# Hybrid decoder block on one core: delta state in another pool, and activation rows padded by one element

## The chip, the cores and the metric

The kernel runs on one core of a Trainium2 chip. The metric is device time in microseconds of one execution. Before the change the median of three runs is 1653.5 us (1650.14 to 1654.55). Engines are named as in the profile: PE does matmuls, PEld its weight loads, DVE vector work, ACT activations and copies, POOL small work, SP issues the DMAs.

## The reference, cut to what matters

One layer on 256 tokens of width 2048, all in float32:

```
mod = silu(c) @ w_ada + b_ada                    # 2048 x 12288: sh1, sc1, gt1, sh2, sc2, gt2
hn  = rmsnorm(x) * (1 + sc1) + sh1
qkv, z, beta, a, glu, gate_a, gate_b = split(hn @ w_in)
A   = gated_delta_net(conv(qkv), beta, a) * silu(z) @ dn_w_o     # 8 heads of 128
B   = silu(layernorm(conv31(val * sigmoid(gl)))) @ cf_w_o        # conformer branch
x   = x + gt1 * ((sigmoid(gate_a) * A + sigmoid(gate_b) * B) @ w_out)
hn  = rmsnorm(x) * (1 + sc2) + sh2
x   = x + gt2 * ((silu(conv3(hn @ w_gate)) * (hn @ w_up)) @ w_down)
out = rmsnorm(x)
```

## The kernel before, in words

Every large product runs through `product` (L283). Its weights come in tiles `w` of 128 x 2 x 512 (512 KB, five buffers). ACT casts each to `wh` (L293), DVE makes the rest `wl` (L295), and PE runs three matmuls per weight slice and token half (L305 to L307): high by high, high by low, high by the weights' low part. The activations hn (later mg, the merged branches, and hn2) stay in one tile of 2 (high, low) x 16 x 256 per partition, and are the operand that PE loads as weights.

The order of the products is: p1 (a first part of all input projections), qkv, glu, gb, z, then **ga** (gate of branch A), **cfo** (`cf_w_o`), **dno** (`dn_w_o`), **out** (`w_out`), and the FFN products up1, gate, up, down. Between their matmuls lie smaller pieces that other bands of the program bring in: the delta rule for two halves of four heads (`delta`, L474), which has a chain of small matmuls and copies for each half, and the conformer's convolution (31 taps per channel on DVE and ACT, L417 to L428) with its layer norm (L758 to L781), which ends in the split `cfh`, `cfl` (L815, L816) that cfo reads.

The modulation `mod` is a side job: a load `ada_w` of one or two rows of `w_ada`, and a DVE sum `ada_acc += ada_w * c_act` (L166) for each. The blocks come in the order gt1 (two blocks of 16 loads of 512 KB), then sc2, sh2 in three parts each, then gt2. For gt1 and gt2 `ada_acc` starts as the bias row (a DMA, L149, after POOL's memset, L147), and PE turns the finished sum into a row with a matmul by ones (L174), which ACT copies to `gt` (L175). `ada_acc` has one buffer, so the next block begins when the last has been read. The side job advances by a credit per weight tile (`side_rate`), and each step is queued on SP behind the weight tile's load that gave it credit. `need` (L215) draws it to its end where a result is used: gt1 before out.

The tag `ada_w` in pool p0 has two buffers. In this order they hold the first q tile of the delta rule (`conv00`, L452), the delta state `St` of the first half (L636), `St` of the second half, and then all `ada_w` loads from gt1 on. The state is written once per half (L637) and read by L612 and L641. Pool pq holds the delta rule's own tiles, among them X0 and X1 (the solved values, L544), U0 and U1; after the delta rule these four tags hold the pieces of gt1 (L803).

A timeline simulation at build time, with bands of priority, sets the order of instructions on each engine; on the chip every engine runs its list in that order, and a buffer is given out in the program's order.

Of the kernel before, what the change touches and what calls it, by code (L numbers as in the profile page):

```python
# [8 lines left out]
F32 = mybir.dt.float32  # L9
F32R = mybir.dt.float32r  # L10
# [4 lines left out]
P = 128  # L15
D = 2048
S = 256
KD = D // P
# [37 lines left out]
def block_kernel(ctx: ExitStack, tc, x, vec, ab, rowv, w_ada, w_in, dn_w_o, cf_w_o, w_out, w_up, w_down, out):  # L56
# [6 lines left out]
    p0 = ctx.enter_context(tc.tile_pool(name="p0", bufs=1))  # L63
# [21 lines left out]
    def turn(out, in_, n=P):  # L85
        nc.tensor.transpose(out=out, in_=in_, identity=ident[0:n, 0:n])  # L86
# [138 lines left out]
    def rstd_col(ss):  # L225

        a = p0.tile([P, 2], F32, tag="nrm_a", name="nrm_a")
        nc.vector.tensor_reduce(out=a, in_=ss, axis=mybir.AxisListType.X, op=ALU.add)
        nc.gpsimd.tensor_scalar(out=a, in0=a, scalar1=1.0 / D, scalar2=EPS, op0=ALU.mult, op1=ALU.add)
        r = p0.tile([P, 2], F32, tag="nrm_c", bufs=3, name="nrm_c")  # L230
        nc.gpsimd.tensor_tensor(out=r, in0=a, in1=mhalf[:, 0:2], op=ALU.pow)
        return r
# [33 lines left out]
    def modulate(part):  # L266
        k0, k1 = R3[part]
        for k in range(k0, k1):
            i = slice(k - k0, k - k0 + 1)
            split(hn, k, x_sb[:, k, :], A1[part][:, i], mod[0][part][:, i])  # L270

    def turned(src, tiles, pool=ps, tag="tp"):

        bank = pool.tile([P, 2, S], F32, tag=tag, name="turned")
        for i, j in enumerate(tiles):
            for t in range(2):
                turn(bank[:, i, t * P:(t + 1) * P], src[:, t, j * P:(j + 1) * P])
        return bank
# [35 lines left out]
    def drain(it):  # L314
        for _ in it:
            pass
# [5 lines left out]
    with b_first():  # L322
        x_sb = p0.tile([P, KD, S], F32, tag="x", name="x_sb")
        xv = x.rearrange("(t p) n -> p t n", p=P)
        xt = p1.tile([P, 2, D], F32, tag="HS", name="xt")
        for q in range(2):
            for t in range(2):
                nc.sync.dma_start(out=xt[:, t, q * 1024:(q + 1) * 1024], in_=xv[:, t, q * 1024:(q + 1) * 1024])
        nc.sync.dma_start(out=vt, in_=vec)
        ss1 = p0.tile([P, 2, 2], F32, name="ss1")  # L330
        for q in range(2):
            for t in range(2):
                sq = p1.tile([P, 1024], F32, tag=("QA", "KA")[t], name="sq")
                nc.scalar.activation(out=sq, in_=xt[:, t, q * 1024:(q + 1) * 1024], func=AF.Square, accum_out=ss1[:, t, q:q + 1])
        r1 = rstd_col(ss1)
        for q in range(4):
            qs = slice(q * 512, (q + 1) * 512)
            for t in range(2):
                nc.vector.tensor_scalar(out=xt[:, t, qs], in0=xt[:, t, qs], scalar1=r1[:, t:t + 1], scalar2=None, op0=ALU.mult)
            for i in range(2):  # L340
                k = 4 * q + 2 * i
                nc.scalar.copy(out=x_sb[:, k:k + 2, :], in_=turned(xt, (k, k + 1), pd, f"dl{i}"))
        for j in (1, 0):
            drain(ada_block(j, 0, sup, 6, shared=True))
        hn = p0.tile([P, 2, KD, S], F32R, tag="hn", name="hn")
        modulate(0)
    hh, hl = (lambda k: hn[:, 0, k, :]), (lambda k: hn[:, 1, k, :])

# [44 lines left out]
    pq = mix.enter_context(tc.tile_pool(name="pq", bufs=1))  # L393
# [75 lines left out]
    def col(t, c, j, hb):  # L469

        i = c * H + hb * 4 + j
        return t[:, i:i + 1]

    def delta(hb, Q, K, Vt):  # L474
# [29 lines left out]
        def big(tag, c):  # L504
            return pq.tile([P, 4, P], F32, tag=f"{tag}{c}", name=f"{tag}{c}")

        def bank(c=""):
            if c == "":
                return ps.tile([P, 4, P], F32, tag="tp", name="bank")
            return pd.tile([P, 4, P], F32, tag=f"dl{c}", name="bank")  # L510

        def tok(c):
            return slice(c * P, (c + 1) * P)
# [93 lines left out]
        St = None  # L607
        for c in range(2):
            if c == 1:
                pt = bank(c)  # L610
                for j in range(4):
                    nc.tensor.matmul(pt[:, j, :], lhsT=K[:, j, tok(c)], rhs=St[:, j, :], start=True, stop=True, skip_group_check=True)  # L612
                for j in range(4):
                    nc.vector.scalar_tensor_tensor(out=X[c][:, j, :], in0=pt[:, j, :], scalar=col(eneg, c, j, hb), in1=X[c][:, j, :], op0=ALU.mult, op1=ALU.add)
            pt = bank(c)
            for j in range(4):
                nc.tensor.matmul(pt[:, j, :], lhsT=U[c][:, j, :], rhs=X[c][:, j, :], start=True, stop=True, skip_group_check=True)
            u = big("T", c)
            for j in range(4):
                nc.scalar.activation(out=u[:, j, :], in_=pt[:, j, :], func=AF.Copy, scale=br[:, c, j:j + 1])  # L620
            po = bank(c)
            for j in range(4):
                nc.tensor.matmul(po[:, j, :], lhsT=A[c][:, j, :], rhs=u[:, j, :], start=True, stop=True, skip_group_check=True)
            o = big("N", c)
            nc.scalar.copy(out=o, in_=po)
            if c == 0:
                pt = bank(c)
                for j in range(4):
                    turn(pt[:, j, :], K[:, j, tok(c)])
                kd = big("P", c)  # L630
                for j in range(4):
                    nc.scalar.activation(out=kd[:, j, :], in_=pt[:, j, :], func=AF.Copy, scale=kds[:, j:j + 1])
                pt = bank(c)
                for j in range(4):
                    nc.tensor.matmul(pt[:, j, :], lhsT=kd[:, j, :], rhs=u[:, j, :], start=True, stop=True, skip_group_check=True)
                St = p0.tile([P, 4, P], F32, tag="ada_w", bufs=2, name="St")  # L636
                nc.scalar.copy(out=St, in_=pt)  # L637
            else:
                pt = bank(c)
                for j in range(4):  # L640
                    nc.tensor.matmul(pt[:, j, :], lhsT=Q[:, j, tok(c)], rhs=St[:, j, :], start=True, stop=True, skip_group_check=True)  # L641
                for j in range(4):
                    nc.vector.scalar_tensor_tensor(out=o[:, j, :], in0=pt[:, j, :], scalar=col(eg, c, j, hb), in1=o[:, j, :], op0=ALU.mult, op1=ALU.add)

            sa = pq.tile([P, 4], F32, tag=f"sa{c}", name="sa")
            junk = big("P", c)
            for j in range(4):
                nc.scalar.activation(out=junk[:, j, :], in_=o[:, j, :], func=AF.Square, scale=so[:, c * 4 + j:c * 4 + j + 1], accum_out=sa[:, j:j + 1])
            nc.gpsimd.tensor_scalar(out=sa, in0=sa, scalar1=1.0 / P, scalar2=EPS, op0=ALU.mult, op1=ALU.add)
            sr = pq.tile([P, 4], F32, tag=f"sr{c}", name="sr")  # L650
            nc.gpsimd.tensor_tensor(out=sr, in0=sa, in1=mhalf[:, 0:4], op=ALU.pow)
            nc.gpsimd.tensor_tensor(out=sr, in0=sr, in1=so[:, c * 4:c * 4 + 4], op=ALU.mult)
            if c == 0:
                on = p1.tile([P, 2, 4, P], F32, tag=("KA", "KB")[hb], name="on")
            for j in range(4):
                nc.scalar.activation(out=on[:, c, j, :], in_=o[:, j, :], func=AF.Copy, scale=sr[:, j:j + 1])
# [92 lines left out]
    with b_delta():  # L749
        on0 = delta(0, *qa)  # L750
# [3 lines left out]
    with b_delta():  # L754
        on1 = delta(1, *qb)
# [67 lines left out]


    side_rate[0] = 0.7
    mg = p0.tile([P, 2, KD, S], F32R, tag="hn", name="mg")
    for g in range(4):
        def evac(pts, g=g):
            for pt, a, b in zip(pts, both(ga, g), both(gb, g)):
# [38 lines left out]
    gt_home[5] = lambda piece: p2.tile([P, 512], F32, tag=f"gt{piece}", name="gt2")  # L868
    with b_first():
        r2 = rstd_col(ss2)  # L870
    hn2 = p0.tile([P, 2, KD, S], F32R, tag="hn", name="hn2")

    def modulate2(part):
        k0, k1 = R3[part]
# [139 lines left out]
```

## Time and profile before

| | us |
|---|---|
| median of three runs | 1653.5 |
| profiled execution, own time | 1656.46 |
| its span, first to last instruction | 1654.8 |
| PE busy | 1530.3 (92%) |
| DVE busy | 1192.5 (72%) |
| ACT busy | 811.3 (49%) |
[...]

PE is busy 92% of the span. A matmul's end is modelled, and matmuls overlap, so a busy PE is not PE at its peak. Some records of matmuls are missing, so counts are a few per cent low in places. DVE and ACT make the split weights ahead of PE, with three buffers each for `wh` and `wl`.

### The profile page before, as it was taken

The numbers are of one execution on the slowest core, as the hardware profiler recorded it, in microseconds if no ns is written. First come the engines' busy times: TensorE is split into PE (matmuls) and PEld (weight loads), VectorE is DVE, ScalarE is ACT, GpSimd is POOL, SyncE is SP. The second block draws the span as 40 slices with busy tenths as digits, with TensorE's granted clock in tenths as the row PEclk, the third lists the DMA queues.
The fourth block names the chain that finished last, engine by engine and source line by source line (L and its number), as shares of the span: only waits on it lengthen the run. The fifth ranks groups of instructions, "written<-read, shape, count | busy, mean of one in ns | idle before, by whom it ended". The sixth has DMA issues, their size and how long they took to land. (4 is left out here: it accounts for less than half of the span.)

```text
span 1654.8 us, 20112 instructions
## 1 busy us (share of the span) xinstructions
PE 1530.3 (92%) x7198; PEld 1257.5 (76%) x7198; DVE 1192.5 (72%) x1556; ACT 811.3 (49%) x1223; POOL 56.4 (3%) x116
## 2 busy tenths in 40 slices
PE   5999999999999997906978999999999999999996
PEld 5887887888887876705867877888888887788885
DVE  5889868699998646846876889987544587755554
ACT  3553436777685644303435633455444444455443
POOL 2000001300021000000000000000000000000000
PEclk9999999999999999957999999999999999999998
DMA  9999765544544446876887988855556777665553
GB/s 341 384 360 356 234 198 145 153 127 138 164 144 132 136 149 208 276 257 220 276 294 264 308 294 291 291 178 175 181 190 196 255 233 246 226 188 183 185 184 101
DMA packets 182860, 366.59 MB, mean 222 GB/s; under 512 B 12516, under 2 KB 30948, under 8 KB 182632
## 3 DMA queue, kind: packets, MB, share of 16 engines
q1 hardware_dynamic: 182760, 365.31, 66.8%
q8 instruction: 56, 0.92, 0.2%
q14 instruction: 44, 0.36, 0.1%
HBM read 363.17 MB, written 2.10 MB: 221 GB/s over the span
## 5 line engine op out<-in xcount | busy, mean ns | idle before, releaser
L293 ACT CAST wh<-w 128x1024 fp32r<-128x1024 f32 x488 | 512.0, 1052 | 565.3 <-PE mm_up L306 133.1
L295 DVE TENSOR_TENSOR wl<-w,wh 128x1024 fp32r<-128x1024 f32 x488 | 593.7, 1222 | 269.3 <-ACT wh L293 267.6
L166 DVE SCALAR_TENSOR_TENSOR ada_acc<-ada_w,c_act,ada_acc 128x768 f32<-128x768 f32 (+2 forms) x236 | 242.9, 1030 | 119.6 <-DMA ada_w<-in_w_ada 113.6
L305 PE MATMUL mm_up<-wh,hn 128*128 128x512 f32 x472 | 185.7, 396 | 0.2 <-ACT hn L263 0.2
L306 PE MATMUL mm_up<-wh,hn 128*128 128x512 f32 x472 | 185.3, 393 | 0.0
L307 PE MATMUL mm_up<-wl,hn 128*128 128x512 f32 x472 | 172.9, 395 | 5.4 <-DVE wl L295 5.2
L305 PE MATMUL mm_down<-wh,h 128*128 128x512 f32 x352 | 139.9, 397 | 0.0
L306 PE MATMUL mm_down<-wh,h 128*128 128x512 f32 x352 | 139.7, 397 | 0.0
L307 PE MATMUL mm_down<-wl,h 128*128 128x512 f32 x352 | 126.4, 397 | 0.0
L305 PE MATMUL mm_p<-wh,hn 128*128 128x512 f32 x280 | 109.7, 395 | 2.1 <-ACT hn L263 2.0
L307 PEld LDWEIGHTS mm_up<-wl,hn 128*128 128x128 f32 x472 | 88.2, 188 | 27.4 <-DVE wl L295 9.4
L306 PE MATMUL mm_p<-wh,hn 128*128 128x512 f32 x280 | 109.0, 391 | 0.0
L305 PEld LDWEIGHTS mm_up<-wh,hn 128*128 128x128 f32 x472 | 89.1, 189 | 18.6 <-ACT hn L263 0.6
L306 PEld LDWEIGHTS mm_up<-wh,hn 128*128 128x128 f32 x472 | 88.7, 188 | 18.3 <-issue 0.5
L307 PE MATMUL mm_p<-wl,hn 128*128 128x512 f32 x280 | 98.7, 393 | 0.9 <-DVE wl L295 0.9
L305 PE MATMUL mm_gate<-wh,hn 128*128 128x512 f32 x232 | 91.3, 394 | 0.0
L306 PE MATMUL mm_gate<-wh,hn 128*128 128x512 f32 x232 | 90.6, 391 | 0.0
L307 PE MATMUL mm_gate<-wl,hn 128*128 128x512 f32 x232 | 85.1, 393 | 0.5 <-DVE wl L295 0.4
L307 PEld LDWEIGHTS mm_down<-wl,h 128*128 128x128 f32 x352 | 66.4, 189 | 16.1
L306 PEld LDWEIGHTS mm_down<-wh,h 128*128 128x128 f32 x352 | 66.4, 189 | 15.9
L305 PEld LDWEIGHTS mm_down<-wh,h 128*128 128x128 f32 x352 | 66.4, 189 | 15.8
L428 DVE SCALAR_TENSOR_TENSOR cfa<-u,vt,cfa 128x256 f32<-128x256 f32 x176 | 75.9, 481 | 0.3
(310 smaller groups left out, 2498.1 us busy)
## 6 DMA issues: line engine op xcount, KB each, us to landing
w<-in_w_up SPq DMA_DIRECT2D x176, 512.0 KB, 4.5
w<-in_w_in SPq DMA_DIRECT2D x130, 512.0 KB, 3.8
ada_w<-in_w_ada SPq DMA_DIRECT2D x96, 512.0 KB, 4.8
ada_w<-in_w_ada SPq DMA_DIRECT2D x128, 384.0 KB, 5.4
w<-in_w_down SPq DMA_DIRECT2D x88, 512.0 KB, 3.6
w<-in_w_in SPq DMA_DIRECT2D x64, 256.0 KB, 4.1
w<-in_w_out SPq DMA_DIRECT2D x32, 512.0 KB, 5.8
w<-in_cf_w_o SPq DMA_DIRECT2D x16, 512.0 KB, 3.5
```

The costliest lines, as they stand in the source:

```text
L166: nc.vector.scalar_tensor_tensor(out=acc[:, 0:n], in0=wt[:, i, :], scalar=c_act[:, k:k + 1], in1=acc[:, 0:n], op0=ALU.mult, op1=ALU.add)
L293: nc.scalar.copy(out=wh, in_=w)
L295: nc.vector.tensor_tensor(out=wl, in0=w, in1=wh.bitcast(F32), op=ALU.subtract)
L305: nc.tensor.matmul(pts[t], lhsT=xh(k)[:, ts], rhs=wh[:, kk, :], start=(k == k0), stop=False)
L306: nc.tensor.matmul(pts[t], lhsT=xl(k)[:, ts], rhs=wh[:, kk, :], start=False, stop=False)
L307: nc.tensor.matmul(pts[t], lhsT=xh(k)[:, ts], rhs=wl[:, kk, :], start=False, stop=(k == k1 - 1))
L428: nc.vector.scalar_tensor_tensor(out=acc[:, i, :], in0=us[g][:, i, k:k + S], scalar=V("cfconv", (2 * g + i) * CFK + k), in1=acc[:, i, :], ...
```

## The change

St is allocated from pool pq under the tag X0 and no longer from p0's `ada_w`. The tiles of hn, mg and hn2 get rows of 257 elements instead of 256, of which the first 256 are used.

```diff
-        hn = p0.tile([P, 2, KD, S], F32R, tag="hn", name="hn")
+        hn = p0.tile([P, 2, KD, S + 1], F32R, tag="hn", name="hn")[:, :, :, 0:S]
...
-                St = p0.tile([P, 4, P], F32, tag="ada_w", bufs=2, name="St")
+                St = pq.tile([P, 4, P], F32, tag="X0", name="St")
...
-    mg = p0.tile([P, 2, KD, S], F32R, tag="hn", name="mg")
+    mg = p0.tile([P, 2, KD, S + 1], F32R, tag="hn", name="mg")[:, :, :, 0:S]
...
-    hn2 = p0.tile([P, 2, KD, S], F32R, tag="hn", name="hn2")
+    hn2 = p0.tile([P, 2, KD, S + 1], F32R, tag="hn", name="hn2")[:, :, :, 0:S]
```

With it the order on the engines moves. SP's queue, at the bias row of gt1's first block (`ada_acc<-in_rowv`), before:

```order
L149 DMA ada_acc<-in_rowv 1x1024
L291 DMA w<-in_w_in 128x2x512 x30
L291 DMA w<-in_cf_w_o 128x2x512 x16
L291 DMA w<-in_dn_w_o 128x2x512 x3
L157 DMA ada_w<-in_w_ada 128x1024
L291 DMA w<-in_dn_w_o 128x2x512
```

And the same place now:

```order
L149 DMA ada_acc<-in_rowv 1x1024
L157 DMA ada_w<-in_w_ada 128x1024
L291 DMA w<-in_w_in 128x2x512 x2
L157 DMA ada_w<-in_w_ada 128x1024
L291 DMA w<-in_w_in 128x2x512 x2
L157 DMA ada_w<-in_w_ada 128x1024
```

The first `ada_w` stood behind 49 weight tiles, and now stands ahead of them; all 32 loads of gt1 lie between the weights of ga, cfo and the first of dno.

On PE, the step from dno to out before (`pt<-ada_acc` is the sum's matmul, `turned<-ident,gb` the transposes of the merged branches):

```order
L305 MATMUL mm_dno<-wh,oh_4863 128x512
L306 MATMUL mm_dno<-wh,ol_4864 128x512
L307 MATMUL mm_dno<-wl,oh_4863 128x512
L174 MATMUL pt<-ada_acc,ones 128x512 x2
L86 MATMUL turned<-ident,gb 128x128 x8
L305 MATMUL mm_out<-wh,mg 128x512 x2
```

The same matmul of that second block of gt1 now, at the step from cfo to dno:

```order
L307 MATMUL mm_cfo<-wl,cfh 128x512
L623 MATMUL bank<-T_4220,G_3878 128x128 x4
L174 MATMUL pt<-ada_acc,ones 128x512
L641 MATMUL bank<-St,conv_3569 128x128 x4
L174 MATMUL pt<-ada_acc,ones 128x512
L305 MATMUL mm_dno<-wh,oh_4845 128x512
```

The pair moved from the end of dno to its start, beside the last reads of St.

On PE, the first use of the layer norm's sum (`pt<-tot,ones_c`, L764) before, in the middle of ga:

```order
L307 MATMUL mm_ga<-wl,hn 128x512
L566 MATMUL bank<-T_3988,N_3842 128x64
L764 MATMUL pt<-tot,ones_c 128x256 x2
L566 MATMUL bank<-T_3988,N_3842 128x64 x3
L86 MATMUL bank<-ident,U_3914 128x128 x4
L305 MATMUL mm_ga<-wh,hn 128x512
```

And now the last rows between ga and cfo, which begin eight rows further up with that L764 (L776 and L251 are the norm's other matmuls, the rest are steps of the delta rule and the first block's L174):

```order
L584 MATMUL bank<-T_4064,N_3842 128x64 x4
L776 MATMUL pt_4277<-ones_c,sqs 128x1 x4
L584 MATMUL bank<-T_4083,N_3890 128x64 x4
L591 MATMUL bank<-U_3866,P_3871 64x64 x4
L251 MATMUL rb<-dg,ones 128x128 x2
L174 MATMUL pt<-ada_acc,ones 128x512
L591 MATMUL bank<-U_3914,P_3919 64x64 x4
L86 MATMUL bank<-ident,U_3866 64x64 x4
L174 MATMUL pt<-ada_acc,ones 128x512
L305 MATMUL mm_cfo<-wh,cfh 128x512 x2
```

The norm's matmuls stood among ga's, with nine more weight tiles of ga behind L764; now all of ga's matmuls stand ahead of them.

## Rows read from the trace of the kernel before

**Rows 1.** The page, busy tenths of the span in 40 equal slices:

```profile
PE   5999999999999997906978999999999999999996
```

**Rows 2.** Line L306: duration ns min/median/max, first and last start us, forms:

```profile
L306 PE MATMUL mm_ga<-wh,hn x128: 387/390/487, 458.4 to 581.1; 128*128 128x512 f32 x128
L306 PE MATMUL mm_out<-wh,mg x128: 388/390/775, 753.3 to 861.5; 128*128 128x512 f32 x128
...
L306 PE MATMUL mm_cfo<-wh,cfl x64: 390/397/484, 581.9 to 635.0; 128*128 128x512 f32 x64
...
L306 PE MATMUL mm_dno<-wh,ol x64: 391/398/775, 649.0 to 701.4; 128*128 128x512 f32 x64
```

**Rows 3.** Timeline of PE: start, us, line, out<-in, xcount [idle before <-releaser]:

```profile
647.37 1.97 PE L86 MATMUL bank<-ident,on 128*128 128x128 f32 x8 [5.58 <-DVE N L643]
...
746.34 3.78 PE L174 MATMUL pt<-ada_acc,ones 128*128 128x512 f32 x4 [44.29 <-DVE ada_acc L166]
...
773.67 1.09 PE L86 MATMUL pt<-ident,ada_acc 128*128 128x128 f32 x4 [9.22 <-DVE ada_acc L166]
...
873.22 1.97 PE L86 MATMUL turned<-ident,xn 128*128 128x128 f32 x8 [10.98 <-ACT xn L877]
```

**Rows 4.** Waits from 700 to 760: us in total, times, longest:

```profile
DVE ada_acc L166 <- DMA ada_w<-in_w_ada: 23.5, 13, 9.1
```

**Rows 5.** Timeline of SP's queue: start, us, what is issued, count:

```profile
481.93 70.25 SPq L291 DMA_DIRECT2D w<-in_w_in  x19
556.76 55.33 SPq L291 DMA_DIRECT2D w<-in_cf_w_o  x16
...
621.88 0.46 SPq L157 DMA_DIRECT2D ada_w<-in_w_ada  x1
...
712.83 44.70 SPq L157 DMA_DIRECT2D ada_w<-in_w_ada  x15
```

**Rows 6.** Busy us by stretch: PE, PEld, DVE, ACT, POOL, clock, DMA, GB/s:

```profile
512.00:572.00 60.00, 60.00 (x347) 52.08 (x346) 47.98 (x75) 36.18 (x60) 1.25 (x2) 1.00 0.43 132
...
641.00:702.00 61.00, 51.98 (x208) 40.72 (x208) 48.73 (x54) 22.25 (x34) 2.35 (x4) 0.92 0.77 253
...
752.00:863.00 111.00, 96.32 (x422) 77.67 (x420) 85.39 (x103) 43.42 (x67) 0.00 (x0) 0.94 0.81 266
...
1500.00:1600.00 100.00, 100.00 (x440) 81.26 (x440) 55.96 (x60) 45.45 (x55) 0.00 (x0) 1.00 0.57 186
```

**Rows 7.** Timeline of PE and DVE along the layer norm:

```profile
540.92 1.08 PE L764 MATMUL pt<-tot,ones_c 128*128 128x256 f32 x4
...
547.22 0.69 DVE L772 TENSOR_TENSOR sqs<-sqs 128x512 f32<-128x512 f32 x1
...
551.81 0.95 PE L776 MATMUL pt<-ones_c,sqs 128*128 128x1 f32 x8
...
553.79 0.29 DVE L250 TENSOR_SCALAR dg<-ident,nrm_r 128x128 f32<-128x128 f32 x1 [0.84 <-POOL nrm_r L243]
...
558.03 0.66 PE L251 MATMUL rb<-dg,ones 128*128 128x128 f32 x4
...
563.87 0.69 DVE L816 TENSOR_TENSOR cfl<-cfa,cfh 128x512 fp32r<-128x512 f32 x1 [1.99 <-ACT cfh L815]
```

**Rows 8.** The sum's group by form, and the landing time of `ada_w` loads:

```profile
L166 DVE SCALAR_TENSOR_TENSOR ada_acc<-ada_w,c_act,ada_acc 128x1024 f32<-128x1024 f32 x64 | 82.1, 1283 | 66.0 <-DMA ada_w<-in_w_ada 62.2 <-DMA ada_acc<-in_rowv 3.7
...
DMA to landing us min/median/max: 3.0/5.2/10.5
```

**Rows 9.** Operands off the raster, and hn's weight loads: ns min/median/max:

```profile
L428 DVE SCALAR_TENSOR_TENSOR cfa<-u,vt,cfa x176: 453/480/493, 333.2 to 536.7; 128x256 f32<-128x256 f32 x176
...
L409 ACT COPY u<-turned x4: 587/590/603, 329.2 to 336.1; 128x512 f32<-128x512 f32 x4
...
L570 PE MATMUL bank<-U,P x128: 217/275/276, 337.6 to 572.0; 128*128 128x64 f32 x128
...
L306 PEld LDWEIGHTS mm_up<-wh,hn x472: 187/188/193, 877.5 to 1526.6; 128*128 128x128 f32 x158
```

## The prediction

> **What bounds the kernel now.** I read the page first, then the table by stage, then the PE timeline where the page shows PE idle, then the waits and the DMA queue there. PE is the bound: it is busy nine tenths or more in nearly every slice, with one hole in slices 17 to 19 and a dent at 21 [rows 1]. In a full stretch 440 matmuls fill 100 us [rows 6], and nothing this change does makes PE's own work smaller, so the time can only come out of the hole.
>
> The stages around it are, by the first and last L306 matmul of each product: ga 458.4 to 581.1, cfo 581.9 to 635.0, dno 649.0 to 701.4, out 753.3 to 861.5 [rows 2]. Between dno and out PE stands still for 44.29 us until `ada_acc` is summed (L174 turns that sum into the row gt1), and in out again for 9.22 us for the next sum; before dno it waits 5.58 us for the delta rule, and before up1 10.98 us for the second norm [rows 3]. The 44 us are no lack of vector speed: inside them DVE itself waits 23.5 us, 13 times, for `ada_w` to land [rows 4]. It waits because all these loads come late. On the queue the weights of ga and cfo go out alone (19 and 16 loads in a row), the first `ada_w` only at 621.88, and then 15 `ada_w` stand ahead of the next `w_out` at 712.83 [rows 5]. Two buffers allow no more than two loads per landing (5.2 us median) plus the sum (1.28 us) [rows 8].
>
> The reason for 621.88: `St` of the second delta half is allocated from the same two-buffer tag ahead of these loads in program order, and it is written at the end of that half. The order of the changed program agrees: with St in another pool the first `ada_w` stands among the first ga weights.
>
> **The change part by part.** I call one weight tile with its 12 matmuls a chunk; ga has 32, cfo and dno 16 each, out 32. Own time of the profiled execution: 1656.5 us (span 1654.8 and 1.7 around it), 3 above the median 1653.5.
>
> A. *ga.* Sixteen `ada_acc` sums of the first gt1 block move into ga, sixteen of the second into cfo. DVE pays 16 x 1.2 = 19 us more in ga (1.28 each less the overlap with the next). By the new order four of them stand only one chunk behind the issue of their load, about 3 us against a landing of 5.2, so DVE also waits some 4 x 2.3 = 9 us with the next weights' split (L295) queued behind. DVE is 80% busy in 512 to 572 [rows 6], so ga's 124 us have 25 us free, and 9 us of layer norm leave ga: 28 against 34. That nearly fits, but the order is fixed and locally uneven: I take 5 us of PE waits, between 0 and 11.5. Against it PE work leaves ga: the norm's matmuls L764, L776, L251 (1.0 to 0.7 us each [rows 7]) and nine groups of four small delta matmuls at about 0.5 us (an estimate from those rows), 7.5 together. A = 5 - 7.5 = -2.5 (-7.5 to +4).
>
> B. *The wait that replaces the old one.* The sums are put among the conformer's taps, so the last tap and the layer norm's `tot` slip from ga's 23rd chunk behind its last. L764 now follows the last ga matmul, and cfo needs the norm's result: PE has little to run meanwhile. Before, the chain ran from 540.92 to the first `cfl` at 564.56 (563.87 + 0.69), hidden in ga. In it L776 stood 3.9 us behind its input (547.91 to 551.81) and L251 3.95 (554.08 to 558.03), behind ga matmuls that are gone now: 23.6 - 7.85 = 15.8 [rows 7]. Then one more thing: PE runs the two L174 of the first block just ahead of cfo, POOL clears `ada_acc` only after them, the bias row is loaded after that, and DVE's first sum of the second block waits for it with the second, third and fourth `cfl` queued behind. This delays cfo's second chunk by about 2 us. B = +17.8; at least 11 (without three splits of 1.2 to 1.5 that stood in the chain), at most 27 (chain not shortened, row later).
>
> C. *cfo.* PE comes out of B at the lower clock, as the 5.58 us gap brings the clock to 0.92 over 641 to 702 [rows 6]; the sums now pace DVE at (5.2 + 1.28)/2 = 3.2 us per load, and cfo's chunks take about 3.3 us on PE (53 us for 16 [rows 2]). +2.2 (0 to 6).
>
> D. *Tail of delta and dno.* The delta steps stand one to three chunks earlier relative to cfo, and six large sums no longer stand between the third and fourth split of dno. [...]
>
> E. *The 44.29 us.* Gone: the second block's last sum stands after cfo's 16th split, and its L174 before dno. With the L174 pair behind the wait (3.78 us, at the low clock) that is 48.1 us, and the pair's work remains elsewhere, about 1.9 at full clock [rows 3]. E = -46.2 (-40, if the last sum, whose load stands behind dno's third weights and so goes out only about two chunks before, makes PE wait at the new place).
>
> F. *out.* 752 to 863 has PE busy 96.3 of 111 us at a mean clock of 0.94 [rows 6]. The 9.22 us go, since that sum now ends in dno four chunks ahead of its transposes, and of 0.06 x 111 / 0.5 = 13 us at half clock about 6 lay in busy time, of which 3 come back. F = -12.2 (-15 to -6).
>
> G. *Padding, and St in X0.* St's write itself takes what it took, and X0's next writer comes after the reads of St are done, some eight chunks later in ga. A hn or mg row is now 257 elements long, so rows start 4 bytes apart from the old raster. Copies into rows of 286 at offset 30 take 590 ns (L409), and DVE reads at every offset from 0 to 30 elements take 453 to 493 ns; a PE moving operand in strided runs takes 217 to 276 [rows 9]. So I cost it 0. What no row shows is a weight load (188 ns [rows 9]) from such an address; it hides under a matmul of 227 ns (100 us / 440 [rows 6]), so up to 39 ns more cost nothing. If that cover were gone, see the slower rival. A gain from it I bound at 0, since weight loads and copies lie under other work already.
>
> Sum: -2.5 + 17.8 + 2.2 - 4 - 46.2 - 12.2 = -44.9. After up1 starts, both orders are nearly alike, and I change nothing there. 1656.5 - 44.9 = 1611.6, less 3 to the median: **1609 us**.
>
> **Rivals.** *Cheaper norm wait.* DVE runs ahead of the order's worst case, B is 11, A -7.5, C 0 and D -8: 6.8 + 5 + 2.2 + 4 = 18 less, 1591. For it: DVE's idle 20% in ga; against: splits are held to three chunks ahead of PE, so DVE can't get far ahead. 15%.
>
> *Dearer norm wait and sums that block the splits.* A +4, B 27, C 6: 1609 + 19.5 = 1628. For it: every `ada_w` wait on DVE holds the splits behind it, as the 13 waits of [rows 4] did. 17%.
>
> *Nothing gained.* The 44 us only change their place: PE loses them at ga's end, in cfo and before dno. Every term would have to stand at its high end at once: 1656.5 - 7 - 3 = 1647; 4%. That St doesn't free the loads is excluded by the order.
>
> *Slower: weight loads from padded rows outgrow their cover.* 4,416 matmuls load weights from hn or mg (1,472 triples of L305 to L307; mm_ga and mm_out have 128 each [rows 2], the rest by the loops), and 15 rows in 16 now start off the old raster: 4,140. Each ns beyond 227 costs 4.1 us; from 238 ns on (4,140 x 11 = 46 us) the gain is eaten. If a load doubled to 376, 4,140 x 149 = 617 us come on top: about 2,230. Against it: no unaligned row of any engine is slower [rows 9]. 6%.
> [...]
>
> **How the numbers follow.** Forecast 58%, cheaper 15%, dearer 17%, nothing gained 4%, slower 6%. About 0.3% (5 us) is what can be told from no change here. The range 1588 to 1638 takes in the forecast, both neighbours and part of their bounds (all low ends: -65.7, all high ends: -7). Faster 0.90, same 0.04, slower 0.06.
>
> **What would show it.** Right: `ada_w` loads from about 450 us on; no PE wait for L174 above some 7 us; a new stretch of 12 to 25 us between ga and cfo in which PE waits on the layer norm (L764 to `cfl`), with a dip of the clock; out begins near 715, up1 near 829 instead of 875; weight loads of hn still near 188 ns. Wrong: a wait for `ada_acc` above 15 us anywhere, ga above 130 us, or hn's weight loads above 227 ns.

## The result and the profile after

| us | before | changed |
|---|---|---|
| median of four runs | 1652.32 | 1603.19 (1601.35 to 1605.7) |
| profiled execution, its span | 1654.8 | 1602.4 |
| PE busy | 1530.3 | 1547.4 |
| mean granted clock, share of full speed | 0.973 | 0.991 |

The changed kernel takes 0.9704 of the time before, 95% interval 0.9683 to 0.9724: 49 us less, where 44.9 were forecast. The sum came out; several of its terms did not, as the experiments show.

The busy tenths of PE and the granted clock over the changed kernel's span, in 40 slices as in [rows 1]:

```profile
PE   5999999999999999999979999999999999999996
...
PEclk9999999999999989999989999999999999999998
```

The hole of slices 17 to 19 is gone; the dent that is left is the second norm ahead of up1. Yet PE is busy 17 us longer than before.

Line L306 of the changed kernel (duration ns min/median/max, first and last start):

```profile
L306 PE MATMUL mm_up<-wh,hn x472: 387/394/795, 821.6 to 1474.4; 128*128 128x512 f32 x158
...
L306 PE MATMUL mm_ga<-wh,hn x128: 387/393/482, 466.4 to 580.0; 128*128 128x512 f32 x128
...
L306 PE MATMUL mm_out<-wh,mg x128: 387/394/481, 709.1 to 804.9; 128*128 128x512 f32 x128
...
L306 PE MATMUL mm_cfo<-wh,cfl x64: 392/397/500, 599.9 to 653.9; 128*128 128x512 f32 x64
...
L306 PE MATMUL mm_dno<-wh,ol x64: 391/397/483, 659.6 to 708.4; 128*128 128x512 f32 x64
```

Against [rows 2] two things are to be seen. The starts give the stages (second table below). And the median duration of every product that loads hn or mg rose, from 389 or 390 ns to between 393 and 396, while cfo and dno kept theirs within 1 ns.

PE's timeline, from the last ga matmul to the first of dno, and the second norm:

```profile
580.48 1.03 PE L764 MATMUL pt<-tot,ones_c 128*128 128x256 f32 x4
...
584.40 1.10 PE L570 MATMUL bank<-U,P 128*128 128x64 f32 x8 [0.72 <-ACT P L567]
585.55 2.07 PE L86 MATMUL bank<-ident,U 128*128 128x128 f32 x8
587.41 1.81 PE L584 MATMUL bank<-T,N 128*128 128x64 f32 x8
589.01 1.81 PE L776 MATMUL pt<-ones_c,sqs 128*128 128x1 f32 x8
...
593.61 1.22 PE L251 MATMUL rb<-dg,ones 128*128 128x128 f32 x4
594.63 1.62 PE L174 MATMUL pt<-ada_acc,ones 128*128 128x512 f32 x2
...
599.19 0.74 PE L305 MATMUL mm_cfo<-wh,cfh 128*128 128x512 f32 x2 [0.93 <-ACT cfh L815]
...
654.32 1.05 PE L623 MATMUL bank<-T,G 128*128 128x128 f32 x8
655.20 1.02 PE L174 MATMUL pt<-ada_acc,ones 128*128 128x512 f32 x2
656.07 1.14 PE L641 MATMUL bank<-St,conv 128*128 128x128 f32 x8
...
658.49 1.31 PE L86 MATMUL bank<-ident,on 128*128 128x128 f32 x8
...
814.35 0.69 PE L86 MATMUL turned<-ident,xn 128*128 128x128 f32 x2 [8.79 <-ACT xn L877]
```

The 44.29 us in front of L174 [rows 3] have no successor: both L174 pairs run without idle time ahead of them. Nor have the 5.58 us ahead of dno: the same L86 follows at 658.49 without a wait. The layer norm (L764 to the first cfo matmul) now lies behind ga, 18.7 us long where 17.8 were forecast, but the profile marks only 0.72 and 0.93 us of idle PE in it: PE works through delta steps, a good part of them at the lower clock (mean granted clock 0.72 from 581 to 599). The busy time by stretch, columns as in [rows 6]:

```profile
581.00:599.00 18.00, 16.49 (x91) 13.49 (x89) 9.12 (x16) 10.55 (x24) 2.45 (x4) 0.72 0.17 59
...
657.00:709.00 52.00, 51.41 (x237) 40.40 (x237) 45.50 (x65) 26.77 (x48) 1.84 (x3) 1.00 0.80 267
709.00:806.00 97.00, 93.13 (x403) 73.20 (x401) 73.76 (x84) 40.04 (x55) 0.00 (x0) 1.00 0.84 289
```

SP's queue from gt1's first bias row on, where the kernel before sent 30 weight loads in a row:

```profile
448.89 0.36 SPq L149 DMA_DIRECT2D ada_acc<-in_rowv  x1
449.30 0.36 SPq L157 DMA_DIRECT2D ada_w<-in_w_ada  x1
452.19 3.09 SPq L291 DMA_DIRECT2D w<-in_w_in  x2
456.11 0.34 SPq L157 DMA_DIRECT2D ada_w<-in_w_ada  x1
```

The first `ada_w` leaves at 449.30, 173 us earlier than before. DVE still waits for such loads, but in small pieces; from 580 to 720 us (total, times, longest):

```profile
DVE ada_acc L166 <- DMA ada_w<-in_w_ada: 12.2, 10, 3.3
```

### The profile page after: what moved, and what is told of

Read it like the earlier page. It is cut to its first block, busy times and chain, and to the rows that moved or that the text cites. A ratio compares the mean times of both kernels' runs of the same rounds, so it can differ in the third digit from the quotient of the medians.

```text
span 1602.4 us, 20092 instructions
## 1 busy us (share of the span) xinstructions
PE 1547.4 (97%) x7198; PEld 1256.9 (78%) x7198; DVE 1189.7 (74%) x1556; ACT 809.8 (51%) x1221; POOL 56.5 (4%) x116
## 4 chain that ended last, share of the span: by engine, by line
PE 85%; DMA 5%; DVE 5%; issue 1%; ACT 1%; POOL 1%; SPq 0%; POOLq 0%; ACTq 0%; DVEq 0%
PE mm_up L307 6%; PE mm_up L305 6%; PE mm_up L306 6%; PE mm_down L306 5%; PE mm_down L305 5%; PE mm_down L307 5%; DMA ada_w<-in_w_ada 4%; PE mm_p L307 4%; PE mm_p L305 4%; PE mm_p L306 4%; PE mm_gate L307 3%; PE mm_gate L306 3%; PE mm_gate L305 3%; PE turned L86 2%; PE mm_ga L307 2%; DVE ada_acc L166 2%
## 5 line engine op out<-in xcount | busy, mean ns | idle before, releaser
L305 PE MATMUL mm_up<-wh,hn 128*128 128x512 f32 x472 | 187.8, 400 | 0.4 <-ACT hn L263 0.4
L306 PE MATMUL mm_up<-wh,hn 128*128 128x512 f32 x472 | 187.6, 397 | 0.0
L306 PE MATMUL mm_down<-wh,h 128*128 128x512 f32 x352 | 139.5, 396 | 0.0
L305 PE MATMUL mm_p<-wh,hn 128*128 128x512 f32 x280 | 111.7, 402 | 2.1 <-ACT hn L263 2.0
L306 PE MATMUL mm_p<-wh,hn 128*128 128x512 f32 x280 | 111.1, 399 | 0.0
L306 PEld LDWEIGHTS mm_up<-wh,hn 128*128 128x128 f32 x472 | 88.8, 188 | 20.9 <-issue 0.5
L306 PE MATMUL mm_gate<-wh,hn 128*128 128x512 f32 x232 | 91.7, 395 | 0.0
L306 PEld LDWEIGHTS mm_down<-wh,h 128*128 128x128 f32 x352 | 66.3, 188 | 16.0
```

Source lines behind the costliest of these rows:

```text
L305: nc.tensor.matmul(pts[t], lhsT=xh(k)[:, ts], rhs=wh[:, kk, :], start=(k == k0), stop=False)
L306: nc.tensor.matmul(pts[t], lhsT=xl(k)[:, ts], rhs=wh[:, kk, :], start=False, stop=False)
```

## The experiments

**The two edits apart.** Each kernel carries one edit only.

```diff
-                St = p0.tile([P, 4, P], F32, tag="ada_w", bufs=2, name="St")
+                St = pq.tile([P, 4, P], F32, tag="X0", name="St")
```

> St moves to X0, the rows of hn, mg and hn2 stay 256 elements long; every engine's order is that of the changed kernel. Theory of the prediction (term G is 0): the same time as the changed kernel, 1603 us, within 5. Rival, from the changed kernel's trace, where matmuls that load hn or mg start 232 ns apart and not 227: without the padding they start 227 ns apart again, and the time is up to 4,416 x 5 ns = 22 us less, so 1581 to 1595.

Measured: 1586.73 us, ratio 0.9598 (0.9578 to 0.9617). The other:

```diff
-        hn = p0.tile([P, 2, KD, S], F32R, tag="hn", name="hn")
+        hn = p0.tile([P, 2, KD, S + 1], F32R, tag="hn", name="hn")[:, :, :, 0:S]
```

(and mg, hn2 likewise)

> The rows are padded by one element, St stays in the modulation's load buffers. Theory of the prediction: 1652 us, no difference to the kernel before. Rival: the padding costs 10 to 22 us wherever St is: 1662 to 1674, with the matmuls that load hn or mg 232 ns apart, and the wait of PE for ada_acc before out still near 44 us.

Measured: 1667.66 us, ratio 1.0088 (1.0066 to 1.0109). PE's timeline with the padding alone still has the old wait ahead of L174:

```profile
753.93 3.78 PE L174 MATMUL pt<-ada_acc,ones 128*128 128x512 f32 x4 [43.07 <-DVE ada_acc L166]
```

So St's new place takes 66 us, and the padding gives back 15 to 17. PE's busy time on the page says the same without any waits in it: 1524.1 us with St alone, 1547.4 with both, 1530.3 before, 1549.8 with the padding alone. 23.3 us more (St alone to both) over the 4,416 matmuls that load hn, mg or hn2 are 5.3 ns each. The time between the starts of two such matmuls, taken from the traces, has its median at 227 ns without the padding and 232 with it. In a stretch of the first product in which PE never rests (60 to 100 us), the kernel before does this:

```profile
60.00:100.00 40.00, 40.00 (x184) 33.34 (x183) 32.36 (x34) 21.08 (x28) 0.00 (x0) 1.00 1.05 377
```

and the changed kernel this, at the same full clock:

```profile
60.00:100.00 40.00, 40.00 (x178) 32.39 (x178) 32.06 (x35) 20.34 (x27) 0.00 (x0) 1.00 1.01 353
```

Six matmuls fewer in 40 us. The span grows by less than 23 us (1588.1 to 1602.4) because PE, when faster, waits longer for DVE and ACT: it is idle for 64.0 us with St alone and 55.0 with both.

**Why the padding costs.** Two things change at once. Each row now starts 4 bytes further off the old raster, the 1,024-byte steps at which rows used to begin; and the tile is 128 bytes longer, which moves all tiles behind it. Two theories follow. By the first the odd starts of the rows cost, and whole rows bring 227 ns and the time of St alone back; by the second it is the place of hn against the tiles that moved. Two kernels, both with St in X0, hold the room and leave the rows whole (mg and hn2 likewise):

```diff
-        hn = p0.tile([P, 2, KD, S], F32R, tag="hn", name="hn")
+        hn = p0.tile([P, 2 * KD * S + 32], F32R, tag="hn", name="hn")[:, 0:0 + 2 * KD * S].rearrange("p (i k s) -> p i k s", i=2, k=KD)
```

> St in X0; hn, mg and hn2 keep rows of 256 elements from the tile's start, and the tile gets 32 unused elements behind its last row, which takes the room that the padding takes. Every tile allocated behind it (w, wh, wl and all later pools) then lies 128 bytes further on, as in the changed kernel, and hn stays where it was. [...] Rival, that the cost depends on where the loaded weights lie against the moving operand (in the kernel before, hn and wh lie on the same address modulo 512 bytes and take 227 ns, all other pairs lie apart and take 234): 234 ns, and as slow as the changed kernel, 1600 to 1608. [...]

With `[:, 32:32 + 2 * KD * S]` in its place:

> As the kernel with 32 unused elements behind the last row, but with the 32 ahead of the first row: hn, mg and hn2 now move on by 128 bytes together with wh and wl. By both theories 227 ns and the time of St alone (1581 to 1595); only if the place of the other tiles matters by itself does it stay near 1603.

Measured: 1597.82 us, ratio 0.9659 (0.9639 to 0.9679), with the unused elements behind; 1587.16 us, ratio 0.9597 (0.9579 to 0.9615), with them ahead. L306 with them behind, then with them ahead:

```profile
L306 PE MATMUL mm_up<-wh,hn x472: 387/393/795, 819.4 to 1472.8; 128*128 128x512 f32 x158
```

```profile
L306 PE MATMUL mm_up<-wh,hn x472: 387/389/793, 810.9 to 1457.6; 128*128 128x512 f32 x158
```

Rows on the old raster, 128 bytes from wh's address, cost 11 of the padding's 16 us of time; moving hn along with wh takes all of it back. By PE's busy time (1546.0 us behind, 1528.2 ahead) the cost is 22 of the 23 us, of which 18 come back, and the median interval is 227 ns again. So it is only in small part the odd start of a row (5 us of time, 1 us of PE's busy time are left for that); most of it hangs on where the operand that PE loads as weights, hn, lies against the operand that moves, wh or wl. If that holds, the products that always took 397 ns should be curable by a shift alone. Three small tiles go in front of hn:

```diff
-    c_act = p0.tile([P, KD], F32, name="c_act")
+    c_act = p0.tile([P, KD], F32, name="c_act"); ss2, ss3 = (p0.tile([P, 2, 4], F32, name=f"ss{i}") for i in (2, 3)); ea = p0.tile([P, H], F32, name="ea")
...
-        ea = small("ea", H)
...
-    ss2, ss3 = (p0.tile([P, 2, 4], F32, name=f"ss{i}") for i in (2, 3))
```

> St in X0, no padding, and three small tiles of 32 bytes each (ss2, ss3, ea) allocated ahead of hn and no longer behind the weight tiles, so that hn, wh and wl move on by 96 bytes and every pool behind them stays: hn, wh, h (down), oh, ol (dno) and cfl (cfo) now all lie on the same address modulo 512 bytes. Theory that a matmul's interval depends on where loaded weights and moving operand lie against each other: the 352 x 3 matmuls of down, the 64 x 3 of dno and about two thirds of cfo's 192 go from 234 to 227 ns, 1,376 x 6.5 ns = 9 us less than St alone (1587): 1578. Rival (234 ns belongs to these products for another reason, such as their tile shapes): 1587.

Measured: 1580.3 us, ratio 0.9555 (0.9533 to 0.9577); its median stands 6.4 us under St alone, its PE busy time 9.1 us (1515.0), as reckoned for the matmuls. Line L306 of down with St alone, and here:

```profile
L306 PE MATMUL mm_down<-wh,h x352: 392/397/403, 1095.0 to 1573.4; 128*128 128x512 f32 x176
```

```profile
L306 PE MATMUL mm_up<-wh,hn x472: 387/389/796, 808.3 to 1452.3; 128*128 128x512 f32 x158
L306 PE MATMUL mm_down<-wh,h x352: 387/389/397, 1090.0 to 1562.0; 128*128 128x512 f32 x176
```

Down now has hn's duration. This is the fastest kernel of the study. The last of this set puts hn 64 bytes away:

```diff
-        hn = p0.tile([P, 2, KD, S], F32R, tag="hn", name="hn")
+        hn = p0.tile([P, 2, KD, S], F32R, tag="hn", name="hn"); ss2, ss3 = (p0.tile([P, 2, 4], F32, name=f"ss{i}") for i in (2, 3))
...
-    ss2, ss3 = (p0.tile([P, 2, 4], F32, name=f"ss{i}") for i in (2, 3))
```

> St in X0, no padding; the two 32-byte tiles ss2 and ss3 are allocated between hn and the weight tiles, so that hn stays and w, wh, wl move on by 64 bytes: hn and wh lie 64 bytes apart, h and wh 32 (96 before). So far distances of 0 and 512 bytes gave 227 ns (256 and 768 too, for 54 matmuls of cfo), and 96, 128 and 352 gave 232 to 234. If only multiples of 256 bytes are cheap: the hn products at 232 to 234 ns, down at 234, and 1597 to 1605, some 10 to 18 us over St alone (1587). If multiples of 64 bytes were cheap (and 128 slow for another reason): 227 ns for hn and 1587.

Measured: 1589.73 us, ratio 0.961 (0.9585 to 0.9634). Neither expectation: hn's matmuls stand 229 ns apart, down's 233. The cost is graded, and 64 bytes below wh cost little.

| address of the loaded weights less that of the moving operand, remainder modulo 256 bytes | 0 | 32 | 96 | 128 | 192 | 128 to 252 in steps of 4 (padded rows) |
|---|---|---|---|---|---|---|
| mean time between two starts, ns | 227.7 | 233 | 234.2 | 232.5 | 229.2 | 233 (229 to 253 for single half rows) |

The addresses are those that the built program gives its tiles, the times are taken from the starts of all neighbouring matmuls of these traces. Modulo 512, the distance 0 rests on some 4,000 matmuls of each kernel, the distance 256 on some 55 of cfo in one kernel (228 ns). The distance isn't the whole rule: padded rows that happen to lie at 192 take some 234, and not 229, and those at 156 and 220 take 244 and 242 (by the matmul that starts the interval), while the other 30 lie between 229 and 236.

A rival is that DVE, ACT or the DMAs, which also read and write `w`, `wh` and `wl`, slow PE at some addresses. The traces speak against it. In down, with DVE, ACT and POOL idle from 250 ns before the first of two starts to the second, the interval is 234.2 ns in the kernel before (23 intervals) and 226.7 with the shifted tiles (20). With no DMA packet under way in the same stretch it is 234.3 (127) and 226.7 (71). Both are the means of all of down.

**What the layer norm's wait costs.** If PE has little to run in it, taking it away should bring most of its length.

```diff
-    side[0], side_rate[0] = ada_blocks([(2, 0), (2, 1), (4, 0), (3, 0), (4, 1), (3, 1), (4, 2), (3, 2), (5, 0), (5, 1)], p0, 2, b_ada), 0.6
+    side[0], side_rate[0] = ada_blocks([(2, 0), (2, 1), (4, 0), (3, 0), (4, 1), (3, 1), (4, 2), (3, 2), (5, 0), (5, 1)], p0, 2, b_ada), 0.2
...
-    side_rate[0] = 0.9
+    side_rate[0] = 1.0
...
-    side_rate[0] = 0.7
+    side_rate[0] = 1.0
```

> St in X0, no padding, and the side job paced at 0.2, 1.0, 1.0 sums per weight tile in ga, cfo and dno instead of 0.6, 0.9, 0.7. The layer norm's matmuls then stand in ga again, L764 six and L251 one weight tile ahead of ga's end, and the second L174 pair in dno behind its 13th tile. Theory of the prediction's term B (PE has little to run while it waits for the layer norm): 12 to 16 us less than St alone, 1571 to 1575. Rival, from the trace of St alone, where PE is busy in 12 of the 15 us ahead of cfo with delta steps and L174 that ga and dno no longer have: only the idle 3 us and some clock come back, 1581 to 1585. Third: gt1 comes late again and out waits for it, over 1590.

Measured: 1602.49 us, ratio 0.9693 (0.9672 to 0.9713), 16 us slower than St alone. The time falls in the third expectation's range, but not for its reason: PE waits for no gt1 sum ahead of out, and out is 93.3 us long against 96.3. The time from ga's last to cfo's first L306 went from 16.6 to 7.5 us (578.4 to 585.9), but ga grew from 112.7 to 120.4, and at the end of cfo PE now waits for the delta rule (from cfo's last to dno's first L306 19.8 us, 5.7 with St alone):

```profile
651.68 2.07 PE L617 MATMUL bank<-X,U 128*128 128x128 f32 x8 [5.77 <-DVE X L614]
654.99 2.08 PE L623 MATMUL bank<-T,G 128*128 128x128 f32 x8 [1.23 <-ACT T L620]
657.74 2.08 PE L641 MATMUL bank<-St,conv 128*128 128x128 f32 x8 [0.68 <-ACT N L625]
```

These small matmuls take 2.07 us where L623 and L641 take 1.05 and 1.14 in the changed kernel: they run at the lower clock, as the stretch says (its third number from the end, 0.62):

```profile
645.00:661.00 16.00, 7.55 (x34) 6.31 (x32) 10.56 (x14) 5.06 (x13) 0.60 (x1) 0.62 0.72 247
```

The same with paces 0.1, 1.2, 1.0:

> As the kernel with paces 0.2, 1.0, 1.0, but 0.1, 1.2, 1.0: the layer norm stands two to three weight tiles earlier still (L251 three tiles ahead of ga's end), and cfo gets 19 sums, more than one per weight tile. If the norm's place against ga's end decides, it is as fast or up to 3 us faster than that one. If the loads for the sums in cfo and dno decide (two buffers, about 5.2 us from issue to landing), cfo becomes longer than 57 us and it is 3 to 8 us slower than that one.

Measured: 1589.95 us, ratio 0.9614 (0.9592 to 0.9637), 12.5 us faster than the paces before; neither expectation. Here the wait ahead of cfo is gone altogether (ga's last L306 at 575.5, cfo's first at 576.4), and the time is 3 us above St alone: ga is 2.8 us longer, cfo 4.0, cfo's end to dno's first L306 16.2 instead of 5.7, dno 1.3 longer, out 3.5 shorter, and up1's first L306 comes at 811.8 instead of 812.8. At the pace 0.1 the norm and the delta rule trade places and their sum stays; at 0.2 PE waits in both places (7.5 and 19.8 us).

With the shifted tiles, the paces 0.2, 1.0, 1.0, and then 0.4, 0.9, 0.7:

> Both of the above at once. If the matmul interval and the layer norm's wait are separate, the two gains add: 9 for the interval and 12 to 16 or 3 to 5 for the wait, so 1563 to 1566 by term B, 1573 to 1575 by its rival.

> The fastest version so far (St in X0, all weight-loaded tiles on wh's address modulo 256) with a pace of 0.4 instead of 0.6 in ga. L764 stands three tiles ahead of ga's end, L776 and L251 still behind it. If delta steps and layer norm only trade places on DVE, as the paces 0.2 and 0.1 showed, the time is that of the fastest version, 1580, within 5; if a shorter chain behind ga's end is worth what it is shorter by, 3 to 6 us less.

Measured: 1593.35 us, ratio 0.9636 (0.9613 to 0.966), and 1588.42 us, ratio 0.9602 (0.9576 to 0.9628). The first is 9 us under the same paces without the shift: the two effects add, but the pace costs where it was to gain, so both its times were missed. The second is 8 us slower than pace 0.6: both expectations missed, and a shorter chain behind ga brought nothing.

**Late loads without St's tie.** No side job in ga (0 in place of 0.6):

> St in X0, no padding, and no step of the side job during ga (0, 0.9, 0.7 per weight tile): the loads can start early, but start with cfo, some 130 us later, a time nearer to that of the kernel before. The layer norm stands in ga again (L764 ten tiles ahead of its end), the second block's L174 pair in out behind its sixth tile. Theory of terms E and F (the wait for ada_acc is a matter of how late the loads go out): a wait for the sums comes back in out, 7 sums at up to 3.2 us each after dno's end less six tiles of 3 us, so 3 to 10 us, with a longer cfo and dno; the wait ahead of cfo goes; in all 1585 to 1600. Rival (the wait came from the state's buffers alone): no wait for ada_acc above 3 us, and with the layer norm's wait gone 1570 to 1580.

Measured: 1614.44 us, ratio 0.9766 (0.9744 to 0.9787), outside both ranges. The wait of terms E and F does not come back: PE waits for no sum ahead of L174 or in out. Late loads cost elsewhere, and more than I expected: the later blocks (sc2, sh2) come late as well, and PE waits for one of them in up1, which is 18.7 us longer (815.1 to gate's first L306 at 1006.0, against 812.8 to 985.0).

```profile
894.06 1.51 PE L86 MATMUL pt<-ident,ada_acc 128*128 128x128 f32 x6 [11.20 <-DVE ada_acc L166]
```

## Why the prediction came out, step by step

The stages by first and last L306 start, changed kernel from the fence above, before from [rows 2], in us of the span; St alone likewise, from:

```profile
L306 PE MATMUL mm_up<-wh,hn x472: 387/389/798, 812.8 to 1460.1; 128*128 128x512 f32 x158
...
L306 PE MATMUL mm_ga<-wh,hn x128: 387/389/486, 459.3 to 572.0; 128*128 128x512 f32 x128
...
L306 PE MATMUL mm_out<-wh,mg x128: 388/389/476, 699.4 to 795.7; 128*128 128x512 f32 x128
...
L306 PE MATMUL mm_cfo<-wh,cfl x64: 392/398/628, 588.6 to 644.2; 128*128 128x512 f32 x64
...
L306 PE MATMUL mm_dno<-wh,ol x64: 392/397/477, 649.9 to 698.7; 128*128 128x512 f32 x64
```

| | before | forecast change | changed | St alone |
|---|---|---|---|---|
| start to ga | 458.4 | 0 (G) | +8.0 | +0.9 |
| ga | 122.7 | -2.5 (A) | -9.1 | -10.0 |
| ga to cfo | 0.8 | +17.8 (B) | +19.1 | +15.8 |
| cfo | 53.1 | +2.2 (C) | +0.9 | +2.5 |
| cfo to the end of dno | 66.4 | -4 (D) | -11.9 | -11.9 |
| dno to out | 51.9 | -46.2 (E) | -51.2 | -51.2 |
| out | 108.2 | -12.2 (F) | -12.4 | -11.9 |
| out to up1 | 16.0 | 0 | +0.7 | +1.1 |
| up1 to the end | 777.3 | 0 (G) | +3.5 | -2.0 |
| sum | | -44.9 | -52.4 | -66.7 |

**E, F: right.** The loads leave at 449, the 44.29 us and the 9.22 us of [rows 3] are gone, and out runs at a clock of 1.00 instead of 0.94 [rows 6]. E was low by 5. The cause is shown by the two edits apart: the padding alone keeps the wait at 43.07, and St's move alone takes it away, its first `ada_w` leaving at 442.66. That late loads with St out of the way bring this same wait back is not shown: without a side job in ga the wait stood in up1.

**B: the length right, the price wrong.** The chain was forecast at 17.8 us and is 18.7 from L764 to cfo. But the step "PE has little to run meanwhile" failed: PE is busy in 16.49 of 18 us, since the delta steps that leave ga are run here. Part of that busy time is the clock of 0.72; with St alone the same stretch has the full clock, and PE is still busy in 14.14 of 17 us:

```profile
572.00:589.00 17.00, 14.14 (x99) 10.87 (x99) 10.14 (x19) 12.32 (x27) 2.73 (x4) 1.00 0.19 62
```

Term A put 7.5 us of work out of ga against 5 us of new waits, -2.5; it is -9 to -10, and PE's idle time in ga did not grow (123 less 120.43 us before, 113 less 111.26 with St alone). In ga, PE before has 670 matmuls and with St alone 597, by stretch:

```profile
458.00:581.00 123.00, 120.43 (x670) 103.13 (x670) 97.80 (x172) 85.38 (x185) 15.24 (x18) 1.00 0.45 137
```

```profile
459.00:572.00 113.00, 111.26 (x597) 94.88 (x595) 104.87 (x172) 72.97 (x157) 12.04 (x15) 1.00 0.68 219
```

A and B together were put at +15.3 and are +10.0 (+5.8 for St alone). Taking the norm's wait away by the pace brought nothing at 0.1 and 0.2: what PE doesn't run there it runs, or waits for, further on. The pace also moves sums into cfo and dno, so the norm's wait by itself wasn't priced.

**D: too small.** -4, bounds -8 to +2, was -11.9. The 5.58 us ahead of dno [rows 3] went whole, and dno runs at 1.00 where 641 to 702 had 0.92 [rows 6]. The rows offered some 19 us: 9 of idle PE (61 less 51.98), and 9.8 at the lower clock (0.08 x 61 / 0.5, the low stretches of that trace being granted 0.50, as from 645 to 651.7). That 4 of them come back is a choice that no run shows; the runs showed the 11.9.

**G: wrong, the largest miss.** It was costed at 0; it costs 15 to 17 us (23.3 us of PE's busy time). The failed step is "So I cost it 0": it asked only how long each operation by itself takes, and put the one open cost under the cover of the matmul ("so up to 39 ns more cost nothing"). The weight load didn't change at all, so the cover was never put to the test, as [rows 9] against the changed kernel shows:

```profile
L306 PEld LDWEIGHTS mm_up<-wh,hn x472: 187/188/194, 821.6 to 1474.2; 128*128 128x128 f32 x158
```

What changed is the interval of the matmuls, from 227 to 232 ns, so the sign I named to look for (loads still near 188 ns) would have passed a padding of any such cost. The trace of before held the hint: in [rows 2] ga and out have a median of 390 ns and cfo and dno of 397 and 398, with the same shape and line. I read the starts of those rows and not their durations, and the 227 ns came from a window that mixes both kinds.
What G did look at, rows that start off the old raster, is the small part: the kernel with whole rows 128 bytes away still loses 11 of the 16 us, 22 of 23 in PE's busy time.

**The rivals.** "Slower: weight loads outgrow their cover" suspected the right edit, but by another mechanism (weight loads, which stayed at 188 ns), with rows off the raster as the cause, and at too high a price. Its "15 rows in 16" names no raster that a run here shows. "Nothing gained" is excluded by E. The cheaper and the dearer norm wait both priced the wrong thing.

So the forecast of 1609 for 1603.19 was luck in its number; it rests on two errors that nearly cancel: the gain of St's move was put 22 us too small, the padding's cost 16 too small. The range held because of this, not because its bounds were right: St alone, 1586.73, lies below its low end of 1588. The sign "out begins near 715" doesn't follow from the terms either: A to E sum to -32.7, which puts out's first L306 at 720.6; it came at 709.1.

What stays open: by what mechanism the distance acts. That it is the relation of hn's address to that of the group `w`, `wh`, `wl`, which always moved together, is shown (hn at the same address is slow with the group 128 bytes on, and fast when both move), and that it holds without the other engines and without DMA; why whole rows at 192 are cheaper than at 32, 96 or 128, and than padded rows at 192, isn't.

## What to carry to other kernels

A wait that vanishes is paid back only in part by the next chain, if the work that leaves one stage fills the wait of another: count the idle time inside a new wait, not its length. Where a change touches a layout, compare durations and start intervals of the same instruction across tiles in the trace of before: here the effect of addresses stood in it (390 ns for ga and out, 397 and 398 for cfo and dno). And split a change of two edits in thought: a sum that comes out may hide two misses.

## What the runs showed of the hardware

In these kernels a 128x512 matmul (operands of type float32r) follows the last after 227 ns when its weights and its moving operand lie at the same address modulo 256 bytes (modulo 512 in all but some 55 cases), and after 229 to 234 ns on average at the other distances tried (229 to 253 for single half rows of the padded tile), while the load of the weights itself takes 188 ns (median) in every kernel of the study. Laying all tiles that these products load as weights on wh's address (modulo 256), with no other change to the work, took PE's busy time from 1524.1 to 1515.0 us.
